# Fetching for two expert units at once by rounded parts of x, with a shorter weight ring and TensorE work in written order

## The chip, the cores and the metric

The kernel runs on one core of one Trainium2 chip. The metric is the device time of one execution in microseconds (us). Three runs of the kernel before took 2396.76, 2397.3 and 2400.31 us; their median is 2397.3 us.

## The reference

Two transformer blocks run one after the other on 256 tokens of width 1024, each with two layers. A layer is a token mixer followed by a mixture of 32 experts, of which each token uses two. The experts are what this change is about; in block 2 they are, cut to the lines that matter:

```python
def second_block(x, ...):
    for l in range(DEPTH):
        mix = _token_mixer(x, ...)
        x = _layernorm(alpha * x + mix, ln1_g[l], ln1_b[l])
        ffn = _hier_moe(x, ...)                      # all in float32
        x = _layernorm(alpha * x + ffn, ln2_g[l], ln2_b[l])

def _hier_moe(h, w_rg, b_rg, w_re, b_re, w_gate, w_up, w_down):
    # best of 4 groups, then the best 2 of its 8 experts, for each token
    ...
    def expert_block(args):                          # EXPERT_FF = 256
        xe, e = args
        hid = jax.nn.silu(xe @ w_gate[e]) * (xe @ w_up[e])
        return hid @ w_down[e]
```

Block 1 has the same shape, with experts twice as wide (512) and an RMS norm instead of the layer norm.

## The kernel before, in words

The program does, in this order: mixer and experts of block 1 for layers 0 and 1, a final norm, then mixer and experts of block 2 for layers 0 and 1. So there are four expert stages, all made by `moe` (L825 to L1045): two of block 1 (about 300 to 752 us and 920 to 1370 us of the profile) and two of block 2 (about 1638 to 1887 us and 2145 to 2400 us).

**Units.** The 32 experts of a stage are taken in 11 units, by the string in `PLACES`: a wide unit "w" holds 2 experts with room for 64 tokens each, a narrow unit "n" 4 experts with room for 32 each; block 2 has "wwwnwnwnnnw". The first 6 experts of block 2 (`fixed`) are known ahead; the others are put in order of their number of tokens by `Ranks`, so their weights can be asked for only when the index row `kidx` (L739) is there. SP, which issues all weight loads, reads it at L766.

**Work of a unit.** The tokens of a unit are *fetched*: a selection matrix `P` (L865, one DVE instruction for each expert and token half) is multiplied on TensorE with the residual stream `x` in 8 pieces of 128 columns (`products`, L871), and ACT applies scale and shift on the way to `xg` (L879). Then `xg` is multiplied with the expert's first weights A (tile `s`, L1003, called s1 here), the activation `hid` is made (L1006, L1007) and transposed (L1010), multiplied with the second weights B (`second`, L920, in two halves of 512 output columns), rounded into two parts `yh` and `yl` on ACT and DVE (L922, L923), and added into the result through `PT` (`combine`, L933). `PT` comes from a transpose of the weighted selection `Pw` (L942, L946) in `back`. In unit n the fetch is for unit n+1, and the second half of the work (B) is for unit n-1. float32 products take two TensorE records for each instruction; those of rounded parts (F32R) take one.

**Order.** A scheduler places the instructions of a stage on each engine by priority, so fetch, s1 and B work of neighbouring units are interleaved; `issue_after` ties single instructions to the one before.

**The weight stream.** SP loads A and B of the units into a ring of slots of 1 MB, taken in turn: 13 constant ones and `EXTRA` more of the stage, 9 in every stage, 22 in all. In block 2 an expert has 2 MB of A and 1 MB of B, so a wide unit has 6 MB, a narrow one 12 MB and a stage 96 MB. SP's order is A0, A1, B0, A2, B1, then, after `kidx`, A3, B2, ..., A8, B7, A9, then a branch (`overfull`, L780) that is taken only if an expert has more than 64 tokens (it is not, here), then B8, A10, B9, B10. From unit 8 on one slot is held back for the residual.

**Start of a stage.** `Head` (L575 to L623) makes the norm's statistics and the router's logits; in block 2 it also subtracts the mean of `x` in place (L619), and the factor 1/sigma goes into `P` (L865) and comes out again in the combine weights `rwp` (L906).

**End of a stage.** `second` of unit 10, its combines, then `last` (L1959 to L1983): residual, layer norm, and in the last layer the output.

Of the kernel before, what the change touches and what calls it, by code (L numbers as in the profile page):

```python
# [51 lines left out]
class Core:  # L52
# [25 lines left out]
    def constants(self, ctx):  # L78
# [31 lines left out]
        self.tok = cp.tile([128, 2, 4], F32, name="tok")  # L110
# [429 lines left out]
class Head:  # L540
# [58 lines left out]
    def finish(self, t):  # L599
# [13 lines left out]
        if self.centred:  # L613
# [5 lines left out]
            nc.scalar.activation(c.x[:, t], c.x[:, t], AF.Identity, bias=c.tok[:, t, 1:2])  # L619
        nc.scalar.activation(c.tok[:, t, 2:3], l[:, 0:1], AF.Exp, scale=0.5)  # L620
# [204 lines left out]
def moe(c, ctx, index, scale, shift, w13, w2, nf, spare, centred, residual, end):  # L825
# [28 lines left out]
    def group(unit, first):  # L854

        e0, n, cap = unit
        P = p.tile([128, 2, 128], F32, name="P", bufs=2)
        P4 = P.rearrange("p t (g s) -> p t g s", s=cap)
        xg = p.tile([128, 8, 128], F32, name="xg", tag="xg", bufs=2)

        def select():
            at = pos if e0 < fixed else places["pos"]
            for t in range(2):
                for i in range(n):
                    selected = nc.vector.tensor_scalar(P4[:, t, i], c.iota[:, :cap], at[:, t, e0 + i:e0 + i + 1],  # L865
                                                       c.tok[:, t, 0:1], op0=ALU.is_equal, op1=ALU.mult)
            return selected

        def products(q, k, start):
            for t in range(2):  # L870
                nc.tensor.matmul(q, x[:, t, k * 128:(k + 1) * 128], P[:, t], start=start and t == 0, stop=t == 1,  # L871
                                 skip_group_check=True)

        def modulate(q, k, vector):
            o = xg[:, k]
# [5 lines left out]
        def fetch(k):  # L881
            def f():
                q = mp.tile([128, 512], F32, name="ms")[:, :128]
                products(q, k, True)
                modulate(q, k, False)
            return f

        def fetch_all():
            qs = [yp.tile([128, 512], F32, name="y", tag="y", bufs=4) for _ in range(4)]
            for k in range(8):  # L890
                q = qs[k % 4][:, (k // 4) * 128:(k // 4 + 1) * 128]
                products(q, k, k < 4)
                modulate(q, k, k % 2)
        return P4, xg, [select] + ([fetch_all] if first else [fetch(k) for k in range(8)])

    P, xg, steps = group(units[0], True)
    selected = steps[0]()
    for f in steps[1:]:
# [6 lines left out]
    wp = p.tile([128, 2, 32], F32, name="rwp")  # L905
    nc.vector.tensor_mul(wp, w, c.tok[:, :, 2:3].to_broadcast([128, 2, 32]))  # L906
# [5 lines left out]
    def second(pr, half, bank="s2"):  # L912
# [4 lines left out]
        for f in range(chunks):  # L917
            for i in range(ne):
                ht, o = (pr["h"][0][:, f], i) if centred else (pr["h"][i // per][:, f % 2], 2 * (i % per) + f // 2)
                nc.tensor.matmul(q[cap * i:cap * i + cap, :], ht[:, o * cap:o * cap + cap],  # L920
# [6 lines left out]
    def combine(pr, halves=(0, 1)):  # L927
        if not y:
            y.extend([[yp.tile([128, 512], F32, name="y", tag="y", bufs=4) for h in range(2)] for t in range(2)])
        for half in halves:  # L930
            for i, part in enumerate(("yh", "yl")):
                for t in range(2):
                    d = nc.tensor.matmul(y[t][half], pr["PT"][:, t, :], pr[part][:, half, :],  # L933
# [4 lines left out]
    def back(pr):  # L938
# [3 lines left out]
        nc.vector.tensor_mul(Pw.rearrange("p t (g s) -> p t g s", s=cap), P,  # L942
                             (wp if e0 < fixed else wk)[:, :, e0:e0 + ne, None].to_broadcast([128, 2, ne, cap]))
        q = mp.tile([128, 512], F32, name="ms")
        for t in range(2):
            nc.tensor.transpose(q[:, t * 128:(t + 1) * 128], Pw[:, t], c.id)  # L946
# [17 lines left out]
    turn = len(units) - 2  # L964
    for n, unit in enumerate(units):
        if n:
            P, xg = nxt[:2]
        nxt = group(units[n + 1], False) if n + 1 < len(units) else (None, None, [])
        e0, ne, cap = unit
        last = n == len(units) - 1  # L970
        todo = nxt[2]
# [8 lines left out]
        if n == turn:  # L980
            begun = first(who, 0)
# [1277 lines left out]
```

## Time and profile before

| what | value |
|---|---|
| median of three runs | 2397.3 us |
| own time of the profiled execution | 2401.7 us |
| its span in the profile | 2399.7 us |
| mean granted TensorE clock | 0.972 |
| PE busy (TensorE matmuls) | 2182.2 us, 91% |
| DVE, ACT busy | 899.4 us (37%), 774.6 us (32%) |
| DMA, bytes moved | 775.20 MB, mean 323 GB/s |

The profiled execution was 4.4 us slower than the median; sums are made against its own time. PE is TensorE's matmul pipe, PEld its weight loads, "PEclk" the granted clock as a share of full speed (1.00 is 2.4 GHz, 0.50 is 1.2 GHz), and "DMA share" the mean busy share of the core's 16 DMA engines. A "PEq" or "SPq" is the sequencer of an engine. Some matmul ends are modelled, so the mean length of a matmul can be longer than the distance from one to the next.

### The profile page before, as it was taken

Reading aid. Unit: us, or ns where it says so; the run is one execution under the profiler, and the core shown is the slowest. Engines: PE = TensorE matmul, PEld = TensorE weight load, DVE = VectorE, ACT = ScalarE, POOL = GpSimd, SP = SyncE. Lnnn points to the kernel's source line nnn. Section 1 sums busy time; section 2 is a strip of 40 time slices with the busy share of each in tenths; the row PEclk is TensorE's granted clock in tenths of the full one; section 3 lists DMA queues with packets and bytes.
Section 4 is the critical chain, followed back from the end, with each engine's and each line's share of the span. In section 5 each row is a group of like instructions: output and inputs, shape, how many; then the busy total and the mean of one; then the engine's idle time right before and its main releaser. Section 6 shows DMA issues by size and latency. Waiting matters only on the chain. (4 is left out here: it accounts for less than half of the span.)

```text
span 2399.7 us, 33892 instructions
## 1 busy us (share of the span) xinstructions
PE 2182.2 (91%) x13034; PEld 1268.5 (53%) x13034; DVE 899.4 (37%) x2095; ACT 774.6 (32%) x1561; POOL 44.7 (2%) x48
## 2 busy tenths in 40 slices
PE   7999899988778989998877899999999899999997
PEld 4667633323225865333222387995444678984443
DVE  3864511111003753111100264984222547961232
ACT  3642311111113452211111254562222435642222
POOL 0001000000000200000000000000000000000000
PEclk8999999999999999999999998999999989999999
DMA  9977489999999347999999971556999923559997
GB/s 392 412 266 318 176 369 421 421 422 421 382 422 419 121 184 286 421 421 421 421 420 384 421 284 55 177 193 240 407 417 371 398 88 128 194 176 371 417 387 280
DMA packets 119852, 775.20 MB, mean 323 GB/s; under 512 B 14186, under 2 KB 15594, under 8 KB 35451
## 3 DMA queue, kind: packets, MB, share of 16 engines
q1 hardware_dynamic: 119674, 772.85, 80.1%
q8 instruction: 109, 1.79, 0.3%
q14 instruction: 69, 0.56, 0.1%
HBM read 771.75 MB, written 1.05 MB: 322 GB/s over the span
## 5 line engine op out<-in xcount | busy, mean ns | idle before, releaser
L1003 PE MATMUL s<-w,xg 128*32 128x512 f32 (+1 forms) x3072 | 577.2, 610 | 43.8 <-DMA w<-A 40.9
L920 PE MATMUL s<-w,ht 128*32 128x512 f32 (+1 forms) x1536 | 340.1, 612 | 37.9 <-DMA w<-B 36.4
L1003 PEld LDWEIGHTS s<-w,xg 128*32 128x32 f32 (+1 forms) x3072 | 131.6, 120 | 307.3 <-issue 199.0
L402 PE MATMUL pj<-hi,wh 128*128 128x256 f32 x864 | 242.8, 284 | 3.4 <-ACT sg L1785 2.3
L403 PE MATMUL pj<-lo,wh 128*128 128x256 f32 x864 | 243.2, 283 | 0.0
L871 PEld LDWEIGHTS ms<-P,x 128*128 128x128 f32 x1280 | 170.0, 195 | 138.5 <-ACT xg L879 75.0
L404 PE MATMUL pj<-hi,wl 128*128 128x256 f32 x864 | 240.1, 283 | 0.0
L923 DVE SCALAR_TENSOR_TENSOR yl<-s,ws,yh 128x512 fp32r<-128x512 f32 x88 | 66.1, 751 | 383.5 <-ACT yh L922 383.5
L871 PE MATMUL ms<-P,x 128*128 128x128 f32 x1280 | 208.2, 294 | 1.2
L920 PEld LDWEIGHTS s<-w,ht 128*32 128x32 f32 (+1 forms) x1536 | 80.1, 121 | 224.3 <-issue 147.3
L397 ACT ACTIVATE wh<-w 128x512 fp32r<-128x512 f32 x248 | 154.3, 630 | 119.4 <-PE pj L403 88.3
L398 DVE TENSOR_TENSOR wl<-w,wh 128x512 fp32r<-128x512 f32 x248 | 167.0, 688 | 49.4 <-ACT wh L397 45.1
L402 PEld LDWEIGHTS pj<-hi,wh 128*128 128x128 f32 x864 | 165.7, 192 | 9.1 <-ACT sg L1785 2.8
L404 PEld LDWEIGHTS pj<-hi,wl 128*128 128x128 f32 x864 | 164.0, 192 | 4.9 <-issue 2.4
L403 PEld LDWEIGHTS pj<-lo,wh 128*128 128x128 f32 x864 | 165.8, 192 | 0.5 <-issue 0.3
L865 DVE TENSOR_SCALAR P<-iota,kpos,tok 128x32 f32<-128x32 f32 (+1 forms) x216 | 49.4, 300 | 305.0 <-PE ms L871 304.9
L922 ACT ACTIVATE yh<-s,ws 128x512 fp32r<-128x512 f32 x88 | 60.5, 687 | 315.6 <-PE s L920 280.2
L1007 DVE TENSOR_TENSOR hid<-hid,s 128x256 f32<-128x256 f32 x66 | 27.7, 419 | 338.2 <-ACT hid L1006 338.1
L1006 ACT ACTIVATE hid<-s 128x256 f32<-128x256 f32 x66 | 25.3, 383 | 383.5 <-PE s L1003 383.2
L365 DVE TENSOR_TENSOR wl<-w,wh 128x512 fp32r<-128x512 f32 (+2 forms) x164 | 111.3, 689 | 100.6 <-ACT wh L364 86.0
L364 ACT ACTIVATE wh<-w 128x512 fp32r<-128x512 f32 (+2 forms) x164 | 99.5, 615 | 115.0 <-PE pj L350 55.9
L879 ACT ACTIVATE xg<-ms,mod,gain 128x128 f32<-128x128 f32 x160 | 72.8, 457 | 148.9 <-PE ms L871 146.0
(624 smaller groups left out, 2719.8 us busy)
## 6 DMA issues: line engine op xcount, KB each, us to landing
w<-A SPq DMA_DIRECT2D x384, 1024.0 KB, 19.1
w<-B SPq DMA_DIRECT2D x128, 1024.0 KB, 19.7
w<-B SPq DMA_DIRECT2D x128, 512.0 KB, 11.9
w<-ada SPq DMA_DIRECT2D x48, 1024.0 KB, 10.7
w<-wi SPq DMA_DIRECT2D x48, 1024.0 KB, 8.0
w<-w SPq DMA_DIRECT2D x26, 1024.0 KB, 16.7
w<-wo SPq DMA_DIRECT2D x16, 1024.0 KB, 7.3
w<-wbr SPq DMA_DIRECT2D x8, 1024.0 KB, 4.8
```

The lines of the kernel that those rows point to most:

```text
L364: nc.scalar.activation(wh[:, :n], w[:, k], AF.Copy)
L365: nc.vector.tensor_sub(wl[:, :n], w[:, k], wh[:, :n].bitcast(F32))
L397: nc.scalar.activation(wh, w[:, k], AF.Copy)
L398: nc.vector.tensor_sub(wl, w[:, k], wh.bitcast(F32))
L402: nc.tensor.matmul(d, wh[:, e], hi, start=k == 0 and ch % 2 == 0, stop=False, skip_group_check=True)
L403: nc.tensor.matmul(d, wh[:, e], lo, start=False, stop=False, skip_group_check=True)
L404: nc.tensor.matmul(d, wl[:, e], hi, start=False, stop=k == nk - 1, skip_group_check=True)
L871: nc.tensor.matmul(q, x[:, t, k * 128:(k + 1) * 128], P[:, t], start=start and t == 0, stop=t == 1, skip_group_check=True)
L879: nc.scalar.activation(o, q, AF.Identity, bias=shift[:, k:k + 1], scale=scale[:, k:k + 1])
L920: nc.tensor.matmul(q[cap * i:cap * i + cap, :], ht[:, o * cap:o * cap + cap], pr["w2"][i][:, half, f * 512:f * 512 + 512], start=f == 0, s ...
L923: nc.vector.scalar_tensor_tensor(pr["yl"][:, half], q, pr["ws"], pr["yh"][:, half].bitcast(F32), op0=ALU.mult, op1=ALU.subtract)
L1003: nc.tensor.matmul(q[cap * i:cap * i + cap, :], xg[:, k, e * cap:(e + 1) * cap], ws[m][:, k, 512 * o:512 * o + 512], start=k == 0, stop=k ...
```

## The change

In block 2 `x` is fully normalized in place, so `P` holds only 0 and 1 and is made by two DVE instructions a unit. `x` is split into a rounded part `xh` (ACT, 128x1024 for each token half) and the rest `xl` (DVE, four subtractions of 128x512), and a fetch multiplies both by `P` as F32R. Units are fetched in groups [0], [1, 2], [3, 4], ..., [9, 10], two at a time with 256 columns. The constant part of `x`'s scale is no longer carried through `tok`, `rwp` and the residual. `EXTRA` is 6 in block 2 (19 slots). In all four stages every TensorE instruction of the units is tied to the one before it (`pe.put`), in the order of the program text, and that text is rearranged.

```diff
@@ Head.finish (block 2 only)
-            nc.vector.tensor_scalar(c.tok[:, t, 1:2], mv[:, 0:1], -1.0, None, op0=ALU.mult)
...
-            nc.scalar.activation(c.x[:, t], c.x[:, t], AF.Identity, bias=c.tok[:, t, 1:2])
-        nc.scalar.activation(c.tok[:, t, 2:3], l[:, 0:1], AF.Exp, scale=0.5)
+            nc.scalar.activation(c.x[:, t], c.x[:, t], AF.Identity, scale=r, bias=nm)
+        else:
+            nc.scalar.activation(c.tok[:, t, 2:3], l[:, 0:1], AF.Exp, scale=0.5)
@@ moe
+    groups = [[0]] + [[n, n + 1] for n in range(1, len(units), 2)] if centred else [[n] for n in range(len(units))]
+    most = 128 * max(map(len, groups))
+    src = (x,)
+    if centred:
+        src = [p.tile([128, 2, 1024], F32R, name=n) for n in ("xh", "xl")]
+        for t in range(2):
+            nc.scalar.activation(src[0][:, t], x[:, t], AF.Copy)
...
+        def put(cls, f, *args, **kw):
+            with tc.issue_after(cls.last.ins) if cls.last is not None else nullcontext():
+                d = f(*args, **kw)
+            cls.last = d if cls.on else None
+            return d
...
+    def lower(t):
+        for i in range(2):
+            d = slice(i * 512, i * 512 + 512)
+            nc.vector.tensor_sub(src[1][:, t, d], x[:, t, d], src[0][:, t, d].bitcast(F32))
...
+                        selected = nc.vector.tensor_tensor(d[:, t], c.iota[:, None, :cap].to_broadcast([128, n, cap]),
+                                                           at[:, t, e0:e0 + n, None].to_broadcast([128, n, cap]),
+                                                           ALU.is_equal)
...
+                pe.put(nc.tensor.matmul, q, src[i][:, t, k * 128:(k + 1) * 128], P[:, t, :m], start=start and t == 0,
+                                 stop=t == 1 and i == len(src) - 1, skip_group_check=True)
...
     selected = steps[0]()
+    if centred:
+        lower(0)
+        with tc.issue_after(selected.ins):
+            lower(1)
...
@@ the loop over units: after s1 and hid
+            if u == 0 and prev is not None:
+                outer(prev, prev["who"])
+                second(prev, 0)
+            half = len(todo) // 2
+            now = todo[:half] if u == 0 else todo[half:]
+            for f in now:
+                f()
+            if u == 1 and prev is not None:
+                combine(prev)
             q = mp.tile([128, 512], F32, name="ms")
...
             if u == 0 and prev is not None:
-                outer(prev, prev["who"])
-                second(prev, 0)
-            half = len(todo) // 2
-            for f in todo[:half] if u == 0 else todo[half:]:
-                f()
-            if u == 0 and prev is not None:
                 second(prev, 1)
-                combine(prev)
...
         back(pr)
+        if centred and prev is not None:
+            combine(prev)
...
-EXTRA = (9, 9)
+EXTRA = (9, 6)
```

How this moves TensorE's instructions is shown at three places. In these rows `P`, `xg`, `ht`, `hid`, `yh` are the tiles named above, `kover`, `kperm` and `places` belong to the ranking of the experts, and a name `s_` with a number is one accumulator of s1 or of `second`; after the change all instructions issued through `pe.put` carry its line, L867.

First, TensorE at the start of a block-2 stage, from the first fetch to the product that gives `kidx` (`ms<-kperm,places`). Before:

```order
L871 MATMUL y<-P,x 128x128 x8
L722 MATMUL ms<-kover,kafter 32x1
L723 MATMUL ms<-kover,lt 32x1
L724 MATMUL ms<-ones,kover 128x1
L871 MATMUL y<-P,x 128x128 x4
L1003 MATMUL s_12465<-w,xg 64x512
L871 MATMUL y<-P,x 128x128 x2
L1003 MATMUL s_12465<-w,xg 64x512 x3
L871 MATMUL y<-P,x 128x128 x2
L1003 MATMUL s_12465<-w,xg 64x512 x5
L737 MATMUL ms<-kperm,places 1x32
```

With the change:

```order
L867 MATMUL y<-P,xh 128x128 x16
L867 MATMUL y<-P,xl 128x128 x8
L722 MATMUL ms<-kover,kafter 32x1
L723 MATMUL ms<-kover,lt 32x1
L724 MATMUL ms<-ones,kover 128x1
L867 MATMUL y<-P,xl 128x128 x6
L867 MATMUL s_12472<-w,xg 64x512 x4
L867 MATMUL y<-P,xl 128x128 x2
L867 MATMUL s_12472<-w,xg 64x512 x7
L737 MATMUL ms<-kperm,places 1x32
```

The fetch of unit 0 has 32 instructions (24, 6 and 2) of 128 columns instead of 16, all but 2 of them ahead of s1, and 11 instructions of s1 stand ahead of the index product instead of 9.

Second, TensorE within the wide units of a block-2 stage. Before, between two units:

```order
L1010 MATMUL ms<-ident,hid 128x128 x2
L871 MATMUL ms<-P,x 128x128 x2
L933 MATMUL y<-yh,PT 128x512 x2
L871 MATMUL ms<-P,x 128x128 x2
L933 MATMUL y<-yl,PT 128x512 x2
L920 MATMUL s_12692<-w,ht 64x512 x4
L871 MATMUL ms<-P,x 128x128 x2
L1003 MATMUL s_12661<-w,xg 64x512 x2
```

With the change, the end of one unit and the first work of the next, narrow one:

```order
L867 MATMUL ms<-ident,hid 128x128 x2
L867 MATMUL s_12724<-w,ht 64x512 x4
L867 MATMUL ms<-P,xh 128x256 x2
L867 MATMUL ms<-P,xl 128x256 x2
L867 MATMUL ms<-P,xh 128x256 x2
L867 MATMUL ms<-P,xl 128x256 x2
L867 MATMUL ms<-ident,Pw 128x128 x2
L867 MATMUL y<-yh,PT 128x512 x2
L867 MATMUL y<-yl,PT 128x512 x2
L867 MATMUL y<-yh,PT 128x512 x2
L867 MATMUL y<-yl,PT 128x512 x2
L867 MATMUL s_12792<-w,xg 32x512 x32
```

The fetch pieces no longer stand between pieces of s1; s1 (x32) stands in one piece, and the four combines follow one another after the transposes of `Pw`.

Third, TensorE at the end of the last stage. Before:

```order
L933 MATMUL y<-yh,PT 128x512 x2
L920 MATMUL s_18942<-w,ht 32x512
L933 MATMUL y<-yl,PT 128x512 x2
L920 MATMUL s_18942<-w,ht 32x512 x7
L933 MATMUL y<-yh,PT 128x512 x2
L933 MATMUL y<-yl,PT 128x512 x2
L920 MATMUL s_18976<-w,ht 64x512 x4
L920 MATMUL s_18988<-w,ht 64x512 x4
L933 MATMUL y<-yh,PT 128x512 x2
L933 MATMUL y<-yl,PT 128x512 x2
L933 MATMUL y<-yh,PT 128x512 x2
L933 MATMUL y<-yl,PT 128x512 x2
```

With the change:

```order
L867 MATMUL y<-yh,PT 128x512 x2
L867 MATMUL y<-yl,PT 128x512 x2
L867 MATMUL y<-yh,PT 128x512 x2
L867 MATMUL y<-yl,PT 128x512 x2
L867 MATMUL s_18693<-w,ht 64x512 x4
L867 MATMUL y<-yh,PT 128x512 x2
L867 MATMUL y<-yl,PT 128x512 x2
L867 MATMUL s_18705<-w,ht 64x512 x4
L867 MATMUL y<-yh,PT 128x512 x2
L867 MATMUL y<-yl,PT 128x512 x2
```

Both halves of unit 10's `second` (the last two `s_` rows) stood together ahead of its combines; with the change each half is followed by its own combines.

## Rows read from the trace of the kernel before

**Rows 1.** Windows, block 2 (time, length, busy per engine (count), clock, DMA share, GB/s).
```profile
1740.00:1760.00 20.00, 19.56 (x124) 8.25 (x124) 4.57 (x14) 5.71 (x12) 0.00 (x0) 1.00 1.02 414
1820.00:1840.00 20.00, 18.08 (x129) 8.70 (x128) 2.59 (x5) 5.11 (x11) 0.00 (x0) 1.00 0.75 283
2320.00:2340.00 20.00, 16.57 (x110) 7.90 (x106) 3.01 (x6) 5.52 (x12) 0.00 (x0) 0.98 0.79 324
2340.00:2360.00 20.00, 19.99 (x138) 9.01 (x130) 2.68 (x5) 5.50 (x12) 0.00 (x0) 0.94 0.98 364
```

**Rows 2.** Windows, block 1's second expert stage, same columns.
```profile
1260.00:1280.00 20.00, 15.96 (x87) 5.71 (x86) 1.51 (x4) 2.78 (x7) 0.00 (x0) 0.82 0.77 306
1300.00:1320.00 20.00, 12.97 (x74) 2.60 (x66) 1.17 (x2) 1.07 (x2) 0.00 (x0) 1.00 1.01 422
```

**Rows 3.** Windows, a stretch of block 2's mixer, same columns.
```profile
1540.00:1560.00 20.00, 20.00 (x178) 20.00 (x177) 19.73 (x39) 10.70 (x19) 0.00 (x0) 1.00 0.55 203
```

**Rows 4.** Groups of instructions by form, 1660 to 1870 us.
```profile
L871 PE MATMUL ms<-P,x 128*128 128x128 f32 x320 | 51.5, 290 | 0.2
```

**Rows 5.** Costliest groups of the page: the rest left over by a rounded part.
```profile
L398 DVE TENSOR_TENSOR wl<-w,wh 128x512 fp32r<-128x512 f32 x248 | 167.0, 688 | 49.4 <-ACT wh L397 45.1
```

**Rows 6.** Timeline of TensorE, 1640 to 1700 us (start, length, line).
```profile
1643.98 3.09 PE L871 MATMUL y<-P,x 128*128 128x128 f32 x16
...
1655.47 0.21 PE L737 MATMUL ms<-kperm,places 32*1 32x32 f32 x2
...
1676.95 0.44 PE L946 MATMUL ms<-ident,Pw 128*128 128x128 f32 x2
...
1696.41 0.44 PE L946 MATMUL ms<-ident,Pw 128*128 128x128 f32 x2
```

**Rows 7.** Windows of 4 us at a start and at the end.
```profile
1644.00:1648.00 4.00, 4.00 (x27) 3.85 (x27) 3.14 (x21) 2.58 (x5) 0.00 (x0) 0.73 0.02 7
1652.00:1656.00 4.00, 4.00 (x21) 1.54 (x21) 1.16 (x5) 0.46 (x1) 0.00 (x0) 1.00 0.00 0
1656.00:1660.00 4.00, 4.00 (x19) 1.47 (x18) 0.41 (x1) 0.38 (x1) 0.00 (x0) 1.00 0.59 190
2380.00:2384.00 4.00, 4.00 (x19) 1.38 (x18) 0.75 (x1) 2.16 (x3) 0.00 (x0) 1.00 0.14 54
```

**Rows 8.** Waits of SP's DMA queue, 1656 to 1830 us (total, times, longest).
```profile
SPq L176 <- PE s L1003: 25.3, 8, 10.6
SPq L766 <- DVE kidx L739: 19.5, 1, 19.5
```

**Rows 9.** DMA issues, 1656 to 1830 us (count, KB, median us to landing).
```profile
w<-A SPq DMA_DIRECT2D x48, 1024.0 KB, 14.1
```

**Rows 10.** Timeline of DVE before the first block-2 stage.
```profile
1638.17 0.21 DVE L615 TENSOR_SCALAR hnm<-hmv,tok 128x1 f32<-128x1 f32 x1 [1.39 <-ACT tok L612]
...
1642.67 0.98 DVE L865 TENSOR_SCALAR P<-iota,rpos,tok 128x64 f32<-128x64 f32 x4
...
1655.72 0.18 DVE L739 CAST kidx<-ms 1x32 int32<-1x32 f32 x1 [1.88 <-PE ms L737]
```

**Rows 11.** Timeline of ACT at the same place.
```profile
1636.91 1.14 ACT L619 ACTIVATE x<-x,tok 128x1024 f32<-128x1024 f32 x1
1637.95 0.19 ACT L612 ACTIVATE tok<-hl 128x1 f32<-128x1 f32 x1
```

**Rows 12.** Chain that ended last, from 2341 us (start, length, what).
```profile
2348.12 17.17 DMA w<-A
...
2365.33 3.65 PE s L1003 x14
...
2379.90 1.89 PE s L920 x8
...
2384.54 0.75 DVE yl L923
2385.29 0.60 DVE x L1959
```

More of the change, by code (lines that the diff above doesn't have):

```diff
@@ L854, in group @@
[L854 to L859, printed above, removed]
-        def select():
-            at = pos if e0 < fixed else places["pos"]
-            for t in range(2):
[L864 to L872, printed above, removed]
+    class pe:
+        last, on = None, False
+        @classmethod
+        def put(cls, f, *args, **kw):
[3 more added lines that the diff above has]
+            return d
@@ new lines, in moe, with group, products @@
+    places = {"pos": pos}
+    def lower(t):
+        for i in range(2):
+            d = slice(i * 512, i * 512 + 512)
+            nc.vector.tensor_sub(src[1][:, t, d], x[:, t, d], src[0][:, t, d].bitcast(F32))
+    def group(ns, first):
+        m = 128 * len(ns)
+        P = p.tile([128, 2, most], F32R if centred else F32, name="P", bufs=2)
+        P4 = [P[:, :, 128 * i:128 * i + 128].rearrange("p t (g s) -> p t g s", s=units[n][2]) for i, n in enumerate(ns)]
+        xg = p.tile([128, 8, most], F32, name="xg", tag="xg", bufs=2)
+        def select():
+            for d, (e0, n, cap) in zip(P4, [units[n] for n in ns]):
+                at = pos if e0 < fixed else places["pos"]
+                for t in range(2):
+                    if centred:
+                        selected = nc.vector.tensor_tensor(d[:, t], c.iota[:, None, :cap].to_broadcast([128, n, cap]),
+                                                           at[:, t, e0:e0 + n, None].to_broadcast([128, n, cap]),
+                                                           ALU.is_equal)
+                        continue
+                    for i in range(n):
+                        selected = nc.vector.tensor_scalar(d[:, t, i], c.iota[:, :cap], at[:, t, e0 + i:e0 + i + 1],
+                                                           c.tok[:, t, 0:1], op0=ALU.is_equal, op1=ALU.mult)
+            return selected
+        def products(q, k, i, start):
+            for t in range(2):
+                pe.put(nc.tensor.matmul, q, src[i][:, t, k * 128:(k + 1) * 128], P[:, t, :m], start=start and t == 0,
+                                 stop=t == 1 and i == len(src) - 1, skip_group_check=True)
@@ L882, in f @@
             def f():
-                q = mp.tile([128, 512], F32, name="ms")[:, :128]
-                products(q, k, True)
+                q = mp.tile([128, 512], F32, name="ms")[:, :m]
+                for i in range(len(src)):
+                    products(q, k, i, i == 0)
                 modulate(q, k, False)
@@ L889, in fetch_all @@
             qs = [yp.tile([128, 512], F32, name="y", tag="y", bufs=4) for _ in range(4)]
[L890 to L893, printed above, removed]
+            for i in range(len(src)):
+                for k in range(8):
+                    q = qs[k % 4][:, (k // 4) * m:(k // 4 + 1) * m]
+                    products(q, k, i, i == 0 and k < 4)
+                    if i == len(src) - 1:
+                        modulate(q, k, k % 2)
         return P4, xg, [select] + ([fetch_all] if first else [fetch(k) for k in range(8)])
-    P, xg, steps = group(units[0], True)
+    P, xg, steps = group(groups[0], True)
     selected = steps[0]()
+    if centred:
+        lower(0)
+        with tc.issue_after(selected.ins):
+            lower(1)
     for f in steps[1:]:
@@ L964, in moe @@
     turn = len(units) - 2
+    pe.on = True
     for n, unit in enumerate(units):
-        if n:
-            P, xg = nxt[:2]
-        nxt = group(units[n + 1], False) if n + 1 < len(units) else (None, None, [])
+        g = next(i for i, ns in enumerate(groups) if n in ns)
+        at_unit = groups[g].index(n)
+        if at_unit == 0:
+            if n:
+                P, xg = nxt[:2]
+            nxt = group(groups[g + 1], False) if g + 1 < len(groups) else (None, None, [])
+            share = -(-len(nxt[2]) // len(groups[g]))
         e0, ne, cap = unit
         last = n == len(units) - 1
-        todo = nxt[2]
+        todo = [nxt[2].pop(0) for _ in range(min(share, len(nxt[2])))]
         pr = {"n": n, "unit": unit, "h": []}
@@ L980, in moe @@
         if n == turn:
+            pe.last = None
             begun = first(who, 0)
```

37 lines of the change are left out of this document (18 added, 19 removed).

## Prediction

> **What bounds the kernel now.** I read the windows first, because the page's 91% busy TensorE is an average over stages with different limits. In a block-2 expert stage both candidates look full: TensorE is busy 19.56 us of 20 and the DMA engines have a share of 1.02 at 414 GB/s [rows 1]. Busy time alone can't say which one holds the other, so the next view is block 1, where the same stream runs with TensorE idle for a third of the time: 12.97 us busy of 20, and still 1.01 and 422 GB/s [rows 2]. So some 420 GB/s is all that the weight stream gives, and block 2 runs at it. The two are close: after `kidx` the stream has 96 - 16 = 80 MB to bring, 2.49 us each at 421 GB/s, 199 us, and 6.6 for the branch (below) make 206; TensorE has ten units at 19.46 us [rows 6] and the rest of unit 0, some 200 to 210. So work taken off TensorE alone finds the other limit at once.
>
> What is left of time that isn't stream? Three places, and the reader should look for a low DMA share. (1) At the start SP waits for `kidx`, 19.5 us [rows 8]; the stream stands at 0.02 and 0.00 and comes back between 1656 and 1660 us [rows 7], right after `kidx` at 1655.72 [rows 10]. (2) Around the branch the rate falls to 283 GB/s in the first layer, and to 324 and 364 in two windows of the second [rows 1]: 20 x (1 - 283/421) = 6.6 us, and 4.6 + 2.7 = 7.3 us. (3) After the last weights: the chain ends with a transfer of A that lands at 2365.29, then TensorE, ACT and DVE alone [rows 12]; DMA share 0.14 in the window from 2380 says that the last B landed at about 2380.6 [rows 7].
>
> **The change part by part.**
>
> *Fetches of two units.* Now 320 records of L871 take 51.5 us for ten units: 5.15 us a unit, 0.161 us a record [rows 4]. With the change a pair needs 8 pieces of 4 F32R products of 256 columns. F32R products of 256 columns fill a mixer window at 178 in 20.00 us [rows 3]: 0.112 us each, so 3.6 us a pair and 1.8 a unit. TensorE saves 3.35 us a unit, 33 us a stage. One unit now follows another after 19.46 us (`Pw` at 1676.95 and 1696.41) [rows 6]; that becomes 16.1, and I add 0.9 for waits that the written order can't fill (a combine that stands behind the rounding of its half): about 17.0. A wide unit's 6 MB take 14.9 us of stream, a narrow one's 12 MB 29.9, so this saving lies beside the stream: **0 us**. The cover is the stream itself, which is full before and after.
>
> *Start.* `kidx` sets when the stream returns, and its product is queued on TensorE behind the fetch of unit 0. Ahead of that: `tok` (1637.95) stands behind the 1.14 us of `x` on ACT, and `hnm` on DVE waits for it until 1638.17 [rows 10, 11]. With the change `tok` goes first: -1.0. But two of the four subtractions stand ahead of the expert choice on DVE, 2 x 0.688 [rows 5]: +1.4; and selecting by two instructions instead of four (0.98 us [rows 10]) gives about -0.5. Sum -0.1. On TensorE, from the first fetch at 1643.98 to the index product at 1655.47 [rows 6] there are 11.5 us of queue. There the fetch goes from 32 records (16 instructions) to 32 F32R instructions of 128 columns, a form that the trace does not have. Bounds: 0.112, the same type with twice the columns; 0.32, the same columns as a float32 instruction of two records. I take 0.161, one record of 128 columns, because an F32R instruction is one record: the fetch costs what it did. Two more s1 instructions stand ahead, four records at 3.65/14 = 0.26 [rows 12]: +1.0. Together **+0.9 us** a stage, between -0.7 (0.112) and +6.0 (0.32). The other two subtractions delay the ranking on DVE by 1.4, which ends under the same TensorE queue.
>
> *Ring of 19 slots.* SP runs ahead: an A transfer lands 14.1 us (median) after its issue [rows 9]. Three slots of 1 MB are 3 x 2.49 = 7.5 us of lead. It already waits eight times, up to 10.6 us, for s1 to give slots back [rows 8], without a gap in the stream. In the wide units at the front TensorE is slower than the stream, so the lead shrinks there; over the first three units a pace of 19.46 - 7.5/3 = 17.0 us makes good for the three slots, and 17.0 is just what I expect. At 18.2 (a third of the saving lost to waits) 3.6 us are missing. I take **+0.8** a stage, from 0 to +3.6. In the narrow units TensorE waits for the stream and gives slots back in time.
>
> *End of a stage.* In the first layer TensorE's last units follow each other without long waits, and with the fetch of unit 10 done before the branch (5.15 us) it comes to the last weights earlier; the end then hangs on their landing. I take **-1.3**, between -5.1 and 0. In the last layer 4.7 us lie between the last landing (2380.6) and the first residual addition at 2385.29 [rows 12]. With the change the combines of the first half, 4 products, stand ahead of the second half's product, about +1.5 us; against that the first residual addition no longer waits behind the last `yl` (2384.54) [rows 12], about -0.6: **+0.9**, from -0.6 to +1.5.
>
> *Block 1.* Only the order changes. The stream is full there [rows 2]; a combine later at the end of a stage: **+0.2** each, between -0.5 and +1.
>
> *The branch.* SP waits there for its own transfers, not for TensorE: 0, between -2 and +2 for both stages together. ACT evicts half as many fetch pieces, twice as wide, and DVE loses the small selections; both have slack: 0.
>
> **Sum:** 2 x 0.9 + 2 x 0.8 - 1.3 + 0.9 + 2 x 0.2 = **+3.4 us** on the profiled execution's 2401.7, so 2405.1. That execution lies 4.4 above the median of 2397.3; against the median I forecast **2400.7 us**. A measurement of this kernel can tell about 0.2%, 4.8 us, from no change; the forecast lies within that.
>
> **A rule against the change.** Row first: after the stand of the branch in block 1 the granted clock is 0.82, while a stretch with TensorE busy only 12.97 of 20 us keeps 1.00 [rows 2]; 1.00 is 2.4 GHz, 0.50 would be 1.2 GHz. The Trainium skill, "TensorE: Matmul & The Clock Gate", section "Why this matters for your kernels", says that waits between bursts of matmuls let the clock drop to half. After the change TensorE waits some 10 us more in each narrow unit. By the row the clock holds and costs nothing; by the rule the work behind the last landing would run at half speed.
>
> **The rivals.**
>
> *The ring starves the stream (slower).* Place: the first narrow unit's weights and those behind it, whose slots come from units 1 to 3. It decides at a pace of 17.0 us a unit: if the written order makes TensorE wait for ACT and DVE at each half, the lead is gone. For it: my pace has no margin. Against it: the median lead of 14.1 us [rows 9] is nearly twice what is taken. Price 3.6 instead of 0.8 in both stages: 2406.3 us.
>
> *Unit 0's products cost as much as float32 (slower).* At 0.32 us `kidx` comes 6.0 later, not 0.9: +10.2 for two stages, 2410.9 us. For it: the columns, not the type, might set it. Against it: rounded products of 256 columns cost a third of that.
>
> *The clock falls in TensorE's waits (slower).* Behind the last landing lie 1.89 us for half a `second` [rows 12] and about as much of combines; at half clock +3.5 a stage, 2407.7 us. Against it the row of 12.97 us.
>
> *TensorE's lead shows at the ends (faster).* F32R at 0.112 (-0.7 instead of +0.9 at both starts), no loss to the ring, the first layer's end at its bound of -5.1 and the last layer's at -0.6: 2 x (-0.7) - 5.1 - 0.6 + 0.4 = -6.7, or 2390.6 us. For it: a lead of 3.35 us a unit is there to be used. Against it: the stream must be let go earlier too, and only `kidx` does that. If even the 414 instead of 421 GB/s [rows 1] were TensorE's doing, 1.7% of 199 us in each stage would go on top, 2383.8; but the share of 1.02 in that row says that the DMA engines had no pause.
>
> *TensorE is the limit after all (faster).* 33 us a stage would go: 2331 us. Rows 2 exclude nearly all of it, since the stream has no more to give. If on the other hand the F32R products of 256 columns ran at the float32 price, TensorE would gain nothing, the ring would cost its 7.5 in full, and the time would be 2397.3 + 3.4 + 2 x 6.7 = 2414 us: the change would not do what it says.
>
> **How the numbers follow.** Forecast 0.44 (nearly all within 0.2%); ring 0.20; float32 price at unit 0 0.08; clock 0.06; no gain at all 0.02; TensorE's lead 0.18; TensorE the limit 0.02. So faster 0.20, within 0.2% 0.44, slower 0.36. The range runs from a little under the faster rival's 2390.6 to the float32 price's 2410.9: 2389 to 2411; outside lie the two extremes, the faster rival's lower end, and the slower ones where they add up.
>
> **What would show it.** Right: DMA share still about 1.0 through the block-2 units while TensorE's busy time there falls by a sixth and waits for `w<-A` appear in the narrow units; `kidx` within 2 us of its place; the branch gaps of the same size; no new gap in the stream among the first five units. Wrong: a window there with a DMA share below 0.95 and SP waiting for s1 (the ring); `kidx` 3 us or more later (the 128-column products); a granted clock below 0.9 in the narrow units; or stages shorter by more than 5 us, which would mean that TensorE held the stream.

## The result, and the profile after

The changed kernel takes 2414.85 us (median of 4 runs, 2413.92 to 2417.64) against 2397.77 us before (4 runs): ratio 1.0073, 95% interval 1.0061 to 1.0086, so 17 us slower. The forecast was 2400.7 us with a range of 2389 to 2411; the result lies above the range and moved by more than three times what can be told from no change. The profiled execution took 2417.64 us, span 2415.9, which is 2.8 us above the median.

Block 1 is not where the time went: in both profiles its second stage ends at the same time (last combine at 1374.18 us before, 1374.26 after). In block 2 the stages were cut at three points of the timelines: F, the first fetch product; K, the end of the `kidx` cast; E, the end of the last combine. In the table below, "filler" is idle TensorE work that the program runs ahead of the expert choice, "index first" means that no s1 stands ahead of the product that gives `kidx`, and each ratio is against runs of the kernel before taken beside that run (their medians lie between 2397.55 and 2398.89 us). The experiments are told behind the table.

| kernel | F to K, layer 0 and 1 | K to E, layer 0 and 1 | median us | ratio to before (95%) |
|---|---|---|---|---|
| before | 11.9, 12.2 | 224.6, 222.2 | 2397.77 | |
| the change | 15.8, 17.1 | 224.2, 226.1 | 2414.85 | 1.0061 to 1.0086 |
| e1 short ring alone | 12.0, 12.5 | 228.7, 229.8 | 2409.17 | 1.0033 to 1.0058 |
| e2 written order alone | 11.8, 11.8 | 224.1, 223.0 | 2403.07 | 1.0013 to 1.0032 |
| e3 change, index first | 8.9, 9.1 | 230.3, 230.7 | 2413.79 | 1.0049 to 1.0075 |
| e4 before, index first | 6.2, 6.1 | 226.0, 226.4 | 2396.76 | 0.9984 to 1.0001 |
| e5 change, start undone | 5.3, 5.3 | 229.5, 228.5 | 2395.77 | 0.9981 to 0.9999 |
| e6 e5, unit 1 alone | 5.6, 5.6 | 228.5, 228.0 | 2398.42 | 0.9999 to 1.0017 |
| e7 e6, index first in block 1 | 5.6, 5.6 | 230.7, 229.9 | 2388.11 | 0.9957 to 0.9980 |
| e8 before, index first in block 1 | 11.5, 12.0 | 222.1, 221.0 | 2393.63 | 0.9972 to 0.9990 |
| e9 change, more filler | 10.5, 10.5 | 224.3, 223.3 | 2399.53 | 0.9993 to 1.0011 |
| e10 e9, index first | 6.1, 6.1 | 230.0, 229.8 | 2403.27 | 1.0006 to 1.0024 |
| e11 e5, index first in block 1 | 5.3, 5.3 | 227.7, 228.0 | 2384.55 | 0.9925 to 0.9952 |
| e12 before, less filler | 10.4, 11.0 | 220.8, 224.8 | 2399.66 | 0.9994 to 1.0012 |
| e13 change, unit 0 float32 | 14.2, 14.1 | 223.5, 222.8 | 2409.36 | 1.0030 to 1.0057 |
| e14 before, more filler | 10.9, 10.9 | 221.2, 222.1 | 2396.09 | 0.9980 to 0.9998 |

F to K and K to E come from one profiled execution each. In the kernels whose work behind K in block 2 is that of the kernel before (before, e8, e12, e14), K to E lies between 220.8 and 224.6 us in layer 0 and between 221.0 and 224.8 in layer 1, so a difference of less than some 4 us between two rows can't be told from none.

In the change `kidx` comes 3.9 and 4.9 us later after the first fetch, and in the second layer the rest of the stage is 3.9 us longer than in the one profile of before as well. F itself stands later behind the end of the stage before (273.1 and 271.7 us against 269.8 and 271.2). The timeline of TensorE at the first start (start, length) answers to [rows 6]:

```profile
1640.08 2.25 PE L167 MATMUL s<-ident,ones 128*128 128x128 f32 x18
1644.72 0.43 PE L657 MATMUL ms<-ras,lt 128*128 128x64 f32 x2 [2.38 <-DVE ras L655]
...
1647.34 3.67 PE L867 MATMUL y<-P,xh 128*128 128x128 f32 x16
1650.81 1.91 PE L867 MATMUL y<-P,xl 128*128 128x128 f32 x8
...
1654.93 3.68 PE L867 MATMUL s<-w,xg 128*64 128x512 f32 x8
...
1659.12 3.65 PE L867 MATMUL s<-w,xg 128*64 128x512 f32 x14
1662.70 0.21 PE L737 MATMUL ms<-kperm,places 32*1 32x32 f32 x2
```

TensorE stands 2.38 us for DVE (`ras`, the expert choice) behind its filler products (ones by the unit matrix, their result unused), line L167. Then the 16 products with `xh` take 3.47 us to the next row, 0.217 us each, and eight records of s1 3.68, twice what e9 below has for them. The index product comes last, at 1662.70. The windows of 2 us say why the fetch is slow (columns as in [rows 1], the clock is the third number from the right):

```profile
1642.00:1644.00 2.00, 0.34 (x4) 0.15 (x2) 1.89 (x6) 0.95 (x2) 0.00 (x0) 1.00 1.02 418
1646.00:1648.00 2.00, 2.00 (x13) 1.76 (x12) 2.00 (x13) 0.00 (x0) 0.00 (x0) 0.50 0.00 0
1656.00:1658.00 2.00, 2.00 (x8) 0.32 (x4) 0.12 (x1) 0.00 (x0) 0.00 (x0) 0.50 0.03 8
1660.00:1662.00 2.00, 2.00 (x11) 0.71 (x8) 0.00 (x0) 0.00 (x0) 0.00 (x0) 1.00 0.00 0
2158.00:2160.00 2.00, 2.00 (x13) 1.76 (x12) 2.00 (x14) 0.04 (x1) 0.00 (x0) 0.50 0.00 0
2172.00:2174.00 2.00, 2.00 (x6) 0.80 (x6) 0.41 (x1) 0.00 (x0) 0.00 (x0) 0.50 0.00 0
2176.00:2178.00 2.00, 2.00 (x12) 0.67 (x12) 0.57 (x2) 0.00 (x0) 0.00 (x0) 1.00 0.15 29
```

The granted clock is 1.00 up to the stand and 0.50 behind it, 1.2 GHz, from about 1645 to 1659 us in the first layer and from 2157 to 2174 in the second, although TensorE is busy for 2.00 us of 2.00. In the kernel before the same stand was 1.66 us, and the clock was low for some 3 us only:

```profile
1644.00:1646.00 2.00, 2.00 (x10) 2.00 (x10) 1.84 (x14) 1.57 (x3) 0.00 (x0) 0.50 0.04 14
1646.00:1648.00 2.00, 2.00 (x19) 1.85 (x18) 1.30 (x7) 1.01 (x3) 0.00 (x0) 0.95 0.00 0
```

What made the stand longer is in the timelines of DVE and ACT, which answer to [rows 10, 11]:

```profile
1642.03 1.29 DVE L876 TENSOR_TENSOR xl<-x,xh 128x512 fp32r<-128x512 f32 x2 [0.31 <-ACT xh L857]
1643.24 0.22 DVE L647 SCALAR_TENSOR_TENSOR rel<-rfar,logits 128x64 f32<-128x64 f32 x1
...
1655.23 0.22 DVE L735 TENSOR_SCALAR kperm<-krow,krank 32x32 f32<-32x32 f32 x1
...
1662.95 0.18 DVE L739 CAST kidx<-ms 1x32 int32<-1x32 f32 x1 [6.83 <-PE ms L737]
```

```profile
1639.81 1.24 ACT L618 ACTIVATE x<-x,hnm,tok 128x1024 f32<-128x1024 f32 x1 [0.28 <-DVE hnm L614]
1640.96 1.99 ACT L857 ACTIVATE xh<-x 128x1024 fp32r<-128x1024 f32 x2
```

The first two subtractions (1.29 us, and 0.31 of waiting for `xh`) stand ahead of `rel`, from which the choice `ras` is made; in e5 below, where they are moved behind `kidx`, the stand is 0.91 us. `kperm` is ready at 1655.45, and its product still waits 7.25 us behind 22 records of s1.

In the units the profile is nearly as forecast. The stream is full where TensorE has become lighter (against [rows 1]), and TensorE now waits for A; SP waits 26.3 us for `kidx` and is held by s1 for 33.9 us, longer than before but at most 11.0 us at a time ([rows 8]). The clock falls to a mean of 0.83 in some windows of the narrow units, one of the forecast's signs of being wrong; the stream stays full in the first of them:

```profile
1740.00:1760.00 20.00, 19.08 (x124) 8.34 (x125) 4.55 (x12) 4.09 (x8) 0.00 (x0) 1.00 1.02 415
1780.00:1800.00 20.00, 15.33 (x82) 6.80 (x86) 7.55 (x10) 4.11 (x8) 0.00 (x0) 0.83 1.02 420
1800.00:1820.00 20.00, 16.14 (x103) 4.55 (x95) 1.17 (x2) 2.42 (x5) 0.00 (x0) 1.00 1.02 414
2340.00:2360.00 20.00, 13.07 (x68) 3.21 (x68) 0.42 (x1) 0.38 (x1) 0.00 (x0) 0.83 0.76 286
```

```profile
SPq L176 <- PE s L867: 33.9, 14, 11.0
SPq L766 <- DVE kidx L739: 26.3, 1, 26.3
```

In the last of these windows the branch's gap is 20 x (1 - 286/421) = 6.4 us, about as in [rows 1]. A pair's product of 256 columns costs 0.12 us at full clock, and two units are 14.5 us apart (`Pw` at 1675.93 and 1690.47), not the 17.0 of the forecast.

### The profile page after: what moved, and what is told of

The parts are those of the page before. It is cut to its first block, busy times and chain, and to the rows that moved or that the text cites. A ratio compares the mean times of both kernels' runs of the same rounds, so it can differ in the third digit from the quotient of the medians.

```text
span 2415.9 us, 33182 instructions
## 1 busy us (share of the span) xinstructions
PE 2114.3 (88%) x12714; PEld 1254.4 (52%) x12714; DVE 885.6 (37%) x2011; ACT 742.1 (31%) x1481; POOL 45.1 (2%) x48
## 5 line engine op out<-in xcount | busy, mean ns | idle before, releaser
L867 PE MATMUL s<-w,xg 128*32 128x512 f32 (+1 forms) x3072 | 559.6, 616 | 102.9 <-DMA w<-A 84.5
L867 PE MATMUL s<-w,ht 128*32 128x512 f32 (+1 forms) x1536 | 329.0, 641 | 82.4 <-DMA w<-B 63.0
L867 PEld LDWEIGHTS s<-w,xg 128*32 128x32 f32 (+1 forms) x3072 | 145.0, 122 | 465.5 <-issue 276.1
L867 PEld LDWEIGHTS s<-w,ht 128*32 128x32 f32 (+1 forms) x1536 | 79.3, 125 | 294.1 <-issue 170.7
L867 PEld LDWEIGHTS ms<-P,x 128*128 128x128 f32 x640 | 81.0, 195 | 53.8 <-issue 28.2
L350 PE MATMUL pj<-wl,hi 128*128 128x512 f32 (+2 forms) x272 | 107.1, 395 | 0.0
L867 PE MATMUL ms<-P,x 128*128 128x128 f32 x640 | 100.3, 296 | 6.3 <-ACT xg L909 1.1
L349 PE MATMUL pj<-wh,hi 128*128 128x512 f32 (+2 forms) x272 | 102.5, 405 | 2.9 <-ACT rt L418 1.6
## 6 DMA issues: line engine op xcount, KB each, us to landing
w<-B SPq DMA_DIRECT2D x128, 512.0 KB, 10.4
```

What stands on the lines that cost most here:

```text
L349: nc.tensor.matmul(qs[t][:, :n], a, wh[:, :n], start=s, stop=False)
L350: nc.tensor.matmul(qs[t][:, :n], a, wl[:, :n], start=False, stop=False)
L867: d = f(*args, **kw)
```

## The experiments

**e1, the ring alone.**

```diff
-EXTRA = (9, 9)
+EXTRA = (9, 6)
```

> The kernel before with EXTRA = (9, 6), so 19 slots in block 2 and nothing else changed. Theory (the start: kidx came 7.2 us later in the first block-2 stage and 12.3 in the second, of which 5 are new there, and the stream is late by that much to the end): the ring costs nearly nothing, 2396 to 2401 us. Rival (the ring starves the stream): most of the 17 us are here, 2406 to 2415 us, with windows of DMA share below 0.95 among the first units.

Measured: 2409.17 us, 11 us slower, as the rival had it. K to E grows by 4.1 and 7.6 us against the kernel before, F to K stays. A window of the first units falls below the share of 0.95 that the forecast had named as a sign of the ring:

```profile
1680.00:1700.00 20.00, 20.00 (x99) 9.06 (x98) 4.46 (x11) 6.50 (x14) 0.00 (x0) 1.00 0.93 362
1700.00:1720.00 20.00, 19.85 (x130) 8.63 (x129) 4.56 (x14) 5.91 (x14) 0.00 (x0) 1.00 0.95 350
```

So with TensorE's old pace three slots are worth some 11 us. But in the change itself K to E did not grow in the first layer at all, so this alone does not explain it: there the stream came back later, and TensorE's pace behind it is faster. The change with 22 slots was not run.

**e2, the written order alone.**

```diff
+    pe.on = True
...
-                combine(prev)
...
+        if centred and prev is not None:
+            combine(prev)
```

> The kernel before with the written order alone: pe.put on every TensorE instruction of the units and the rearranged loop in all four stages, float32 fetches of one unit, 22 slots. Theory of the start: order costs only the end of the last stage (2.4 us in the trace of the change) and a small shift of kidx, 2398 to 2403 us. Rival (the written order costs TensorE's time through waits for ACT and DVE): 2408 to 2418 us, since TensorE had no idle time in the block-2 stages of before.

Measured: 2403.07 us, 5 us slower and at the upper end of the expectation. Neither F to K (11.8, 11.8) nor K to E (224.1 and 223.0) shows more than 1 us of it a stage. The profiles can't show it: the profiled execution of the kernel before (2401.7 us) lies 4.4 us above its median, that of e2 (2402.8) 0.3 below its own, so the two differ by 1.1 us only. Where the 5 us lie is not settled.

**e3 and e4, the index product first.** In e3 the chain of the written order begins at the index product, in e4 the first s1 of unit 0 is tied to it:

```diff
-        nc.tensor.matmul(q[0:1, 0:E], num, self.perm, start=True, stop=True)
+        self.product = nc.tensor.matmul(q[0:1, 0:E], num, self.perm, start=True, stop=True)
...
     pe.on = True
+    if centred:
+        pe.last = ranks.product
```

> The changed kernel, but in block 2 the first s1 instruction of unit 0 is issued after the product that gives the index row, so no s1 stands ahead of it. Its input kperm was ready at 1655.45 and the product ran at 1662.70 behind 22 records of s1. Theory of the start: kidx 7 us earlier in both stages and the time 12 to 15 us lower, 2400 to 2403 us. Rival (ring or order): kidx earlier, but the stream then waits for slots or TensorE is late, 2409 to 2415 us.

> The kernel before with the same edit: in block 2 no s1 ahead of the index product (kperm was ready at 1649.2, the product ran at 1655.47). If the stream alone bounds the stages: kidx and all behind it 6 us earlier twice, 2386 us. If TensorE, which had no idle time there, bounds them just as much: 2394 to 2399 us, with SP waiting longer for slots. The second would mean that the fetch by two units is what makes an earlier index worth anything.

Measured: 2413.79 and 2396.76 us. `kidx` came 6 to 8 us earlier behind F in both kernels, and nearly nothing was gained: K to E grew by 6.1 and 4.6 us in e3 and by 1.4 and 4.2 in e4 (whose profiled execution, 2392.84 us, was the lowest of its runs). In e3 SP then waited 39.8 us in all for s1 (33.9 in the change), up to 11.0 us at a time; so the theory of the late index fell. The reading of these waits, argued and not tested: what the stream needs behind A3's first slots is s1 of unit 1, done and its slots free, and that hangs on when TensorE gets there. The clock of e3 was at 0.50 for as long as in the change.

**e5 and e6, the start undone.** Unit 0 is fetched from `x` in float32, the subtractions come after `kidx`, and the index product comes first; e6 also fetches unit 1 alone in float32.

```diff
+        whole = centred and first
+        parts = (x,) if whole else src
...
-    if centred:
-        lower(0)
-        with tc.issue_after(selected.ins):
-            lower(1)
...
+    if centred:
+        with tc.issue_after(ranks.ready.ins):
+            lower(0)
+            lower(1)
```

> The changed kernel with its block-2 start undone as far as TensorE and DVE go: unit 0 is fetched in float32 from x, the four subtractions for xl come after kidx, and no s1 stands ahead of the index product; pairs, written order and 19 slots stay. Theory now (two faces of one thing: TensorE comes late to s1 of unit 1, whose slots the stream needs, and only a ring with three more slots hides that): s1 of unit 1 ends 4 to 5 us earlier than with the index first alone, and of the stream's extra loss there (5.6 and 8.4 us from restart to the end of the stage) half goes: 2403 to 2408 us. Rival (the ring alone sets it, whatever TensorE does): 2409 to 2414 us as in the kernel before with the short ring. Rival (the start alone): 2396 to 2400 us.

> The same, and unit 1 is fetched alone too, in float32; pairs begin with units 2 and 3. So only 8 float32 pieces (5.1 us) stand between s1 of units 0 and 1 instead of a pair's 8 (7 us and more in the trace of the index first), and s1 of unit 1 ends another 2 to 4 us earlier. Theory: 2395 to 2401 us, the short ring then costs little, and most of the 17 us are back. Rival (ring alone): 2409 to 2414 us, no change against the run beside it.

Measured: 2395.77 us, 19 us below the change and 2 below the kernel before, and 2398.42 us. With 19 slots, pairs and written order in place, the whole loss was gone; e5 came out lower than its theory, where its rival (the start alone) had it, and e6, which should have been faster still, was 3 us slower. So the cause is in the start, and more than s1 of unit 1 a little earlier. In e5 TensorE stood 0.91 us instead of 2.38, and the clock was 1.00 from the stand to `kidx` in both layers:

```profile
1641.50 0.43 PE L657 MATMUL ms<-ras,lt 128*128 128x64 f32 x2 [0.91 <-DVE ras L655]
```

Three things are undone at once in e5, so it doesn't say which of them counts. It gave the theory of the clock, which the next runs test alone.

**e9 and e10, the clock alone.** Nine more filler products bridge TensorE's stand; nothing else is touched (e10 adds the index product first).

```diff
-    c.warm(sp.tile([128, 512], F32, name="s1")[:, :128], 9, c.routed)
+    c.warm(sp.tile([128, 512], F32, name="s1")[:, :128], 18 if centred else 9, c.routed)
```

> The changed kernel with 18 instead of 9 filler products (ones by the unit matrix, their result unused) on TensorE ahead of the expert choice of block 2, where TensorE stood 2.4 us for DVE and the granted clock was 0.50 from 1646 to 1658 us and from 2158 to 2174 us. Nothing else is changed. Theory (the wait for DVE, longer by the subtractions, costs the clock, and at 1.2 GHz the fetch and s1 of unit 0 take twice as long): clock 1.00 there, first fetch to kidx 11 to 12 us instead of 15.8 and 17.1, time 2403 to 2408 us. Rival (the 128-column rounded products are slow by themselves, 0.23 us): clock 1.00, but first fetch to kidx still 14 us or more, 2411 to 2416 us.

> The same, and in block 2 no s1 stands ahead of the index product. With the clock kept, kidx some 6 us after the first fetch and s1 of unit 1 done 4 to 5 us earlier than with the index first at half clock. Theory of the clock: 2396 to 2402 us, close to the kernel whose unit 0 is fetched in float32 (2395.8). If float32 at unit 0 was what helped there, and not the clock: 2408 to 2414 us.

Measured: e9 2399.53 us, 15 us less than the change, some 4 below what its theory said, and the same as the kernel before (1.0002). Its TensorE timeline and windows at the first start, against those of the change above:

```profile
1639.05 4.26 PE L167 MATMUL s<-ident,ones 128*128 128x128 f32 x36
1643.69 0.43 PE L657 MATMUL ms<-ras,lt 128*128 128x64 f32 x2 [0.37 <-DVE ras L655]
...
1645.44 2.00 PE L867 MATMUL y<-P,xh 128*128 128x128 f32 x16
1647.28 1.06 PE L867 MATMUL y<-P,xl 128*128 128x128 f32 x8
...
1649.71 1.94 PE L867 MATMUL s<-w,xg 128*64 128x512 f32 x8
...
1655.53 0.21 PE L737 MATMUL ms<-kperm,places 32*1 32x32 f32 x2
```

```profile
1646.00:1648.00 2.00, 2.00 (x20) 2.00 (x20) 2.00 (x17) 0.90 (x3) 0.00 (x0) 1.00 0.00 0
1652.00:1654.00 2.00, 2.00 (x11) 0.71 (x12) 0.00 (x0) 0.46 (x1) 0.00 (x0) 1.00 0.00 0
```

The stand is 0.37 us, the clock 1.00 up to K, the 16 products take 1.84 us, 0.115 each, and F to K is 10.5 us in both layers. The rival, that the 128-column products are slow by themselves, is out: 0.115 us is their price at 2.4 GHz. The gain doesn't come from less work ahead of the index product: 24 records of s1 stand ahead of it in both layers, 22 and 18 in the change. e10 was 4 us slower than e9 and missed both of its ranges: the index came 4.4 us earlier behind F, TensorE then stood for `kperm` (0.76 us), the clock fell again (0.54 and 0.60 from 1652 to 1656 us), and K to E grew by 5.7 and 6.5 us. So float32 at unit 0 may have helped e5 (2395.77) beyond the clock; that was not separated.

**e13, what holds the clock down.** The change with unit 0 in float32, the subtractions left where they are.

> The changed kernel with unit 0 of block 2 fetched in float32 from x, and nothing else changed: the subtractions stay ahead on DVE, so TensorE's stand of 2.4 us stays, 9 filler products. If the rounded products behind the stand held the clock down: 1.00 again 2 to 4 us after the fetch begins, as in the kernel before, and 2400 to 2405 us. If the stand alone did: 0.50 for 10 us and more as in the change, and 2410 to 2416 us.

Measured: 2409.36 us. TensorE's stand is 2.39 us as in the change, and the clock falls as there, but it is back at about 1648.8, 3.7 us after the fetch begins (at 1645.09), where the change needed 12:

```profile
1644.00:1646.00 2.00, 2.00 (x13) 1.76 (x12) 2.00 (x15) 0.00 (x0) 0.00 (x0) 0.50 0.00 0
1648.00:1650.00 2.00, 2.00 (x13) 1.33 (x11) 1.65 (x9) 1.59 (x5) 0.00 (x0) 0.81 0.00 0
1650.00:1652.00 2.00, 2.00 (x14) 1.31 (x14) 0.51 (x3) 1.40 (x3) 0.00 (x0) 1.00 0.04 8
```

In the second layer it is back 3.6 us after F too, where the change needed 15. So both count: the stand lets the clock fall, and how long it stays down differs with what TensorE runs behind it. What in the products makes the difference was not tried. The time fell by 5 us only, to a place between the two ranges of the expectation; a reason that the trace shows is that in this kernel all 32 records of s1 came to stand ahead of the index product (F to K 14.2).

**e12 and e14, the controls on the kernel before**: 2 and 18 filler products instead of 9.

> The kernel before with 2 instead of 9 filler products at the same place of block 2, so that TensorE stands for some 3.4 us instead of 1.7. If a longer stand there costs the clock for a dozen us: 0.50 through the fetch of unit 0, kidx 3 to 5 us later in both stages, TensorE and the stream late by it to the end, 2403 to 2409 us. If the clock at that place is not what matters: 2396 to 2400 us.

> The control: the kernel before with 18 instead of 9 filler products in block 2. There the clock was at 0.50 for only some 3 us in the first stage. If the filler gives back only what the clock had cost: 2394 to 2398 us, 0 to 4 us less. If it helps by something else: as much as in the change, 2383 to 2388 us.

Measured: 2399.66 and 2396.09 us. In e14 there is no stand, and the clock is 1.00 from the filler to K in both layers; two windows of the first:

```profile
1644.00:1646.00 2.00, 2.00 (x17) 1.93 (x18) 2.00 (x19) 1.09 (x4) 0.00 (x0) 1.00 0.08 31
1646.00:1648.00 2.00, 2.00 (x15) 1.04 (x14) 1.37 (x9) 1.85 (x3) 0.00 (x0) 1.00 0.00 0
```

More filler gives the kernel before 2 us, not 15, so in the change it gave back what the clock had cost. At full clock F to K of the kernel before is 10.9 us in both layers. Less filler cost nothing that can be told: the stand was 3.23 us and the clock at 0.50 from 1642 to 1648 us, but it was back within 2 us of F, in the float32 fetch. A stand with float32 work behind it is cheap here; the theory of this run missed.

**e7, e8 and e11, the index first in block 1.** TensorE is not full there ([rows 2]), so the thought was that an earlier `kidx` can be used.

```diff
-    if centred:
-        pe.last = ranks.product
+    pe.last = ranks.product
```

> The same, and the index product goes ahead of s1 in block 1 too. There the ring has 22 slots, kperm was ready at 300.1 us and the product ran at 304.86, and TensorE has idle time later on. Stream-bound: about 4.7 us less in each of the two block-1 stages, 8 to 10 us below the run beside it. If slots, not the index, bound the restart: no difference.

> The kernel before with the index product ahead of s1 in block 1 only. The same 4.7 us in each of two stages: 2387 to 2391 us if the stream bounds block 1, 2396 to 2400 us if slots do. Beside the same edit in block 2, which gave 1.3 us, it shows whether TensorE's full time in block 2 was the reason.

> The candidate: the changed kernel with unit 0 of block 2 fetched in float32, xl after kidx, pairs as in the change, and the index product ahead of s1 in all four stages. The same without block 1 took 2395.8 us, and block 1 gave 4 and 10 us in the two kernels that had it: 2385 to 2390 us, below both kernels.

Measured: 2388.11, 2393.63 and 2384.55 us. F to K in block 1 falls from 10.9 to 5.7 and 5.5 us. On the kernel before (e8) K to E gives 3.5 and 3.8 us of it back, so the gain stays below the forecast; with e6 below it (e7) only 0.6 and 1.7. The difference between those two block-1 stages was not followed up. e11, that is e5 with this edit, is the version that beats both: ratio to the kernel before 0.9939, interval 0.9925 to 0.9952, 14 us less than before and 30 less than the change.

## Why the prediction was wrong

**The step that failed is the start.** It counted instructions on DVE and on TensorE and came to +0.9 us a stage, at most +6.0. From the statistics of the last part of `x` to the end of the `kidx` cast the start grew by 5.0 us in the first layer and 6.4 in the second. Its DVE part was about right: `ras` comes 7.5 us after those statistics begin, 6.7 before, so +0.8 where the step had +0.4 (-1.0 and +1.4). What it did not ask is what TensorE does in the meantime. It stood 0.7 us longer, and the clock then stayed at half for 14 and 17 us, in which the fetch and a good part of s1 of unit 0 took twice as long. Between the change and e9, where the edit is the filler alone, F to K shrinks by 5.3 and 6.6 us, 11.9 together; the two short products and the second filler between `ras` and F shrink by 0.9 and 0.7; and K to E of the second layer by 2.8, which is within what single profiles differ by. That is 16 of the 18 us between the two profiled executions (15 between the medians).

**The rule was weighed at the wrong place.** The Trainium skill, "TensorE: Matmul & The Clock Gate", section "Why this matters for your kernels", says that waits between bursts, where they are long enough, cost the clock. The prediction looked for those waits in the narrow units and behind the last landing and gave the rival 0.06 and 3.5 us a stage. In the narrow units the clock was 1.00 with TensorE busy 16.14 of 20 us and fell in single windows only (0.83 from 1780 to 1800 and from 2340 to 2360, 0.91 from 1820 to 1840 and from 2300 to 2320). The sign "a granted clock below 0.9 in the narrow units" was there, but the DMA share was 1.02 in the first of these windows, so the stream set the pace, and K to E of e9 shows no loss that can be told. At the start, where a wait was made longer by the change's own edit and every product behind it lies on the path to `kidx`, the trace agrees with the rule's direction: 2.38 us of standing, then 0.50 (and 1.66, then 0.50 for a shorter time, in the kernel before). The row that could have warned was at hand: 0.73 from 1644 to 1648 us in the kernel before [rows 7] said that the clock was already falling at that place.

**The price of the 128-column products** was bounded by 0.112 and 0.32 and taken as 0.161. It is 0.115 at full clock (e9) and 0.217 at half; the lower bound was right, the choice between was not. With the clock kept F to K is 10.5 us, 1.4 to 1.7 shorter than in the kernel before, where the step had it longer; 1.0 to 1.3 of that is the clock of the kernel before, which has 10.9 at full clock (e14). The sign that the prediction gave to a high price, `kidx` 3 us or more later, came true (3.9 and 4.9 behind F) by another cause. That its case "no gain at all" also came to 2414 us is chance: it needs the 256-column products at the float32 price, and they cost 0.12 us.

**The ring** was sized at +0.8. For itself it costs 4.1 and 7.6 us against the kernel before (e1), or 6.5 and 7.3 against the mean of the four kernels with the same work behind K, near the 7.5 us of lead in the step. In the change with its clock it costs nothing that can be told: K to E in e9 is 224.3 and 223.3 against 224.6 and 222.2, and the change itself has no window of 20 us from 1680 to 1820 or from 2200 to 2340 with a DMA share below 0.99. The likely reason is that units follow each other after 14.5 us, below the 17.0 from which the step said it would be made good. That mechanism fits, with a larger margin than forecast; no run has the change with the long ring, so its share is argued.

**The rest.** The fetch by pairs took work off TensorE and, as far as K to E can tell, nothing off the time; the branch's gap stayed; block 1 ended at the same time. The ends of the stages, +0.9 and -1.3 in the forecast, are too small to be told in K to E. With the clock kept, e9's 2399.53 us lies 1.2 us from the 2400.7 of the forecast. That closeness is partly luck: in e9 F to K is shorter by 3.1 us in the two stages together, where the forecast had the start longer by 1.8, and against the runs of before beside it e9 is 0.6 us slower, not 3.4.

## What to carry to other kernels

Where an edit puts work on one engine ahead of a chain that TensorE waits for, look at the granted clock around that wait, and count everything behind it on the path at half clock as a bound. A few idle filler products that reach to the end of the wait are a cheap test of it, and here brought the whole loss back. An earlier release of the stream gave little by itself here: the index first alone took about 1 us off the change (e3) and the kernel before (e4), and in e3 and e10 K to E grew by more than half of what F to K had lost. And compare single profiles only beyond their spread, which was 4 us a stage here.

## What was not expected of the hardware

With TensorE busy in every window the granted clock stayed at 0.50 for 14 us (1645 to 1659) and 17 us (2157 to 2174) behind a stand of 2.4 us, when rounded products of 128 columns came first; e3, with the same stand and products, had the same lengths. Behind the same stand it was back 3.7 us after F when float32 products came first (e13). Rounded products don't always do so: later in e9, behind a stand of 1.09 us, rounded products of 256 columns ran, and the clock was at 0.50 for only some 3.4 us, from about 1660.8 to 1664.2:

```profile
1660.37 0.66 PE L751 MATMUL ms<-kperm,kT 32*128 32x32 f32 x4 [1.09 <-DVE kT L748]
1660.96 0.80 PE L867 MATMUL ms<-P,xh 128*128 128x256 f32 x2
```

```profile
1662.00:1664.00 2.00, 2.00 (x10) 1.90 (x10) 0.00 (x0) 1.13 (x2) 0.00 (x0) 0.50 1.02 422
1664.00:1666.00 2.00, 1.65 (x11) 1.11 (x9) 0.00 (x0) 1.33 (x4) 0.00 (x0) 0.94 1.02 430
```

What decides how long it lasts is open. Nor does the length of the stand alone say whether the clock falls: it fell behind 0.76 us (e10) and held behind 0.91 us (e5). Rounded products of 128 columns cost 0.115 us each at full clock, as much as those of 256 columns in [rows 3].
